# Mixers of the later chunks in another order, and the first query unit in two column parts

## The chip, the cores and the metric

The kernel runs on one core of one Trainium2 chip. The metric is the device time of one execution in microseconds (us); the median of several runs is compared. The profile is one execution, recorded by the hardware profiler. Engines: PE (TensorE, matmuls), PEld (its weight loads), DVE (VectorE), ACT (ScalarE), POOL (GpSimd, which issues the indirect gathers), SP (SyncE, which issues most plain transfers).

## The reference

One decoder layer, for 512 tokens of a prompt and 32 sample tokens (8 sequences of 4). All numbers are float32.

```
proj = x @ w_in + b_in;  q, k, v, g, ca, cg = split(proj, 6)      # D = 1024, each part 512 wide
o, r_new = retention(rope(q), rope(k), v, r0)                     # 4 heads of 128, chunks of 128 tokens
ret_out  = silu(g) * head_norm(o)
conv_out = silu(layer_norm(depthwise_conv31(ca * sigmoid(cg))))
x = layer_norm(ALPHA * x + concat(ret_out, conv_out) @ w_out)     # "mix" and LayerNorm 1
# retrieval of experts, per token:
q = (x @ w_query) as 8 heads of two halves of 128
s1, s2 = q1 @ sub_keys_1, q2 @ sub_keys_2                         # 128 keys each
take the 16 best of each, then the 16 best of their 256 sums: idx = e1*128 + e2, gate = softmax
y = sum over heads and 16: gate * gelu(u[idx] . x) * v[idx]       # 16384 experts, rows u and v of 1024
x = layer_norm(ALPHA * x + y)
```

Outputs are both token sets, the new retention states and the new convolution caches.

## The kernel before, in words

The program is written as straight Python with generators. A scheduler that simulates times then sets the order on each engine; the text gives it dependencies, priorities and a few forced orders. `behind(a, b)` forces only that `a` is issued after `b` on its engine.

*Tokens.* The first 128 prompt tokens are carried through the mixer and the retrieval early. Each of them has 8 x 16 = 128 expert slots. The other 416 tokens are the 32 samples (`NS`, columns 0 to 32) and three chunks of 128 (`C`), at columns `c0` = 0, `NS`, `NS + C`, `NS + 2C`. Their LayerNorm output is kept transposed in `x1T` (1024 x 416).

*Slots of the first 128 tokens* (`gather0`, function `gather`). For slot k, POOL gathers 128 rows of `uv` into a tile `g` (L667; u in the first half, v in the second). DVE takes the dot with x (L673), ACT makes gelu and the gated weight (L684, L685), and DVE adds weight * v to `acc` (L690). Slots up to 47 have four tiles, later ones three. The slots fill the time of other work. `hold(k, ins)` sets that the dots of slot k and later are issued behind instruction `ins`, such as the last one of a head norm (`steps["p"]`) or a LayerNorm (`steps["ln"]`).

*Mixers.* For each chunk: `retain` (scores, output and state of the retention; `advance` adds to the state `Rst`, L416, and `head_norm` makes `on`, L370), `gate_heads` (transposes of `on` at L377, product with the gate at L378), `mix_a` (the residual by a matmul with a scaled identity, L517, then 32 matmuls with `w_out`, L530: for each of two banks the convolution half first, then the gated half), and `mix_b` (LayerNorm 1 at L498 to L512, transposes into `x1T` at L553, a copy of the chunk to `x_dram`). The samples have a mix of their own, `mix_s` (L541).

*Retrieval of the 416 tokens.* For each pair of heads a "query unit" (`project`, L215) multiplies 4 x 8 blocks of `w_query` by the 416 columns of `x1T`. The result goes to `qs`; key scores (L584) and the top 16 (first MAX8 at L571) follow. The last 256 tokens are not gathered but dense: `scores_of` (L931) multiplies all expert rows `ut` by `x1T`, the chosen gates are scattered to a dense table by matmuls of one-hot tables (M, A, B, L1027 to L1058, products Ga to Gd), and `v_products` (L1115) multiplies the table with all rows `uv`. The samples ("Is", 32 slots) and the next 128 tokens ("Ib", 128 slots) are gathered like the first ones, from slot 30 of Is on only behind the `fence`, the end of the first scatter (`first_keys`). Slots are counted here through all three lists: 0 to 127 are the first tokens', 128 to 159 Is, from 160 on Ib.

*Queues and places.* SP issues the weight loads in program order; `wp` has four 1 MB places for them. `sel` is the pool of the first retrieval's scratch tiles, and of one tile `keys` of 128 x 2048 that serves as room for states and for the sums of two chunks. The room tile is kept by name `room`; `xr0` and `states` are 128 x 1024 tiles of another pool. PSUM (the matmul results) has eight banks, two groups `ps` and `ps0` given out in turn in the mixers.

Of the kernel before, what the change touches and what calls it, by code (L numbers as in the profile page):

```python
# [8 lines left out]
F32 = mybir.dt.float32  # L9
# [6 lines left out]
AF = mybir.ActivationFunctionType  # L16
# [4 lines left out]
D = 1024  # L21
# [76 lines left out]
def tile_step(ctx: ExitStack, tc: tile.TileContext, a, o):  # L98
# [5 lines left out]
    gw = ctx.enter_context(tc.tile_pool(name="gw", bufs=3))  # L104
    wps, right = ExitStack(), ExitStack()
    wp = wps.enter_context(tc.tile_pool(name="wp", bufs=4, side="right", reuse_waits="tile"))
    sel = [right.enter_context(tc.tile_pool(name="sel", bufs=2, side="right"))]
    dr = ctx.enter_context(tc.tile_pool(name="dr", bufs=1, space=bass.MemoryType.DRAM))
    front = ExitStack()
    gx = front.enter_context(tc.tile_pool(name="gx", bufs=1, reuse_waits="tile"))  # L110
# [199 lines left out]

    def conv_norm(y, n):

        pm = mmps()
        for m in range(4):
            T.matmul(pm[:, :n], onesm, y[:, m, :n], start=(m == 0), stop=(m == 3))
        pv = mmps()
        for m in range(4):
            V.tensor_sub(y[:, m, :n], y[:, m, :n], pm[:, :n])
            sq = small("sg", [128, 416], bufs=1)
            S.activation(sq[:, :n], y[:, m, :n], AF.Square)  # L320
            T.matmul(pv[:, :n], onesm, sq[:, :n], start=(m == 0), stop=(m == 3))
        rs = small("ropeB", [128, 416], bufs=1)
        S.activation(rs[:, :n], pv[:, :n], AF.Sqrt, bias=eps_c)
        V.reciprocal(rs[:, :n], rs[:, :n])
        for m in range(4):
            last = V.tensor_mul(y[:, m, :n], y[:, m, :n], rs[:, :n])
            S.activation(y[:, m, :n], y[:, m, :n], AF.Silu, bias=cg_b[:, m:m + 1], scale=cg_g[:, m:m + 1])
        return last
# [45 lines left out]
    def gate_heads(on, gT, c0):  # L374
        pt = mmps().rearrange("p (h t) -> p h t", h=H)
        for h in range(H):
            T.transpose(pt[:, h], on[:, h * DH:(h + 1) * DH], ident)  # L377
        V.tensor_mul(gT[:, :, c0:c0 + C], gT[:, :, c0:c0 + C], pt)  # L378
# [141 lines left out]
    def mix_mm(gT, y, c0, wo, xT=None):  # L520

        banks_ = [mmps(), mmps()]
        if xT is not None:
            for q in range(2):
                residual(banks_[q], xT, range(q * 4, q * 4 + 4), c0)
        for q in range(2):
            for src, k0 in ((y, 4), (gT, 0)):
                for s in range(2):
                    for k in range(4):
                        last = T.matmul(banks_[q][:, s * 256:(s + 1) * 256], src[:, k, c0:c0 + C],  # L530
                                        wo[q * 2 + s][:, k0 + k, :], start=(xT is None and k0 == 4 and s == 0 and k == 0),
                                        stop=(k0 == 0 and s == 1 and k == 3), skip_group_check=True)
        return banks_, last
# [10 lines left out]
            c = slice(j * 256, (j + 1) * 256)  # L544
            V.scalar_tensor_tensor(x1[:NS, c], x1[:NS, c], ALPHA, p[j * NS:(j + 1) * NS, 0:256], op0=OP.mult, op1=OP.add)

    def mix_norm(x1, n, x1T, c0, src=None):

        layer_norm(x1, n, ln1[0], ln1[1], src)
        for q in range(2):  # L550
            pt = mmps().rearrange("p (k t) -> p k t", k=4)
            for k in range(4):
                last = T.transpose(pt[:, k, :n], x1[:n, (q * 4 + k) * 128:(q * 4 + k + 1) * 128], ident[:n, :n])  # L553
            S.activation(x1T[:, q * 4:q * 4 + 4, c0:c0 + n], pt[:, :, :n], AF.Copy)
        return last

    def keys_or_scratch():
        return sel[0].tile([128, 2 * D], F32, name="keys", bufs=1)

    keys = []  # L560

# [168 lines left out]
    n = NR  # L730
# [55 lines left out]
    for h0 in range(0, PH, 2):  # L786
        w = load_w(a["w_query"], h0 * 256)
        qq = small("qe", [128, 4, 128], bufs=1)
        for hs in ([h0], [h0 + 1]) if h0 == 0 else ([h0, h0 + 1],):
# [43 lines left out]
    rope(load_win(1), 1, xT, n - NS, 160, [(0, n - NS, kT)])  # L833
    wg = load_win(3)
    S.activation(y[:, :, s_], yS, AF.Copy)
    hold(47, conv_norm(y, n))
    banks[:] = [ps0]
    ons = {}

    def before(c):  # L840
        c0 = C * (c - 1)
        return scores(qT, kT, c0), k_tokens(kT, c0)
# [6 lines left out]

    retain(1, *before(1))  # L850
    retain(2, *before(2))
    hold(48, steps["p"])
    banks[:] = [ps]
    silu_gate(wg, xT, n - NS, [(0, n - NS, gT[:, :, r])], False)
    wo = load_w(a["w_out"], 0) + load_w(a["w_out"], 512)
# [1 line left out]
    banks[:] = [ps, ps, ps0, ps, ps0, ps, ps, ps0]  # L857
    xrs, pms, room = {}, {}, keys_or_scratch()

    def mix_a(c0, m, place):  # L860
        xrs[c0] = fe.tile([128, D], F32, name="xr0") if place is None else room[:, place * D:(place + 1) * D]
        if c0:
            pms[c0], _ = mix_mm(gT, y, c0, wo, x1T)
            return
        x1, pms[c0] = xrs[c0], None
        nc.scalar.dma_start(x1[:m], a["x"][128:128 + m])
        mix_s(x1, gT, y, wo)

    def mix_b(c0, m):
        mix_norm(xrs[c0], m, x1T, c0, pms[c0])  # L870
        if c0 < NG2:
            nc.sync.dma_start(x1_dram[c0:min(c0 + m, NG2)], xrs[c0][:min(m, NG2 - c0)])

    gate_heads(ons[1], gT, NS)
    third = before(3)
    caches()
    mix_a(0, NS, None)
    retain(3, *third)
    hold(52, steps["p"])
    gate_heads(ons[2], gT, NS + C)  # L880
    mix_a(NS, C, 0)
    gate_heads(ons[3], gT, NS + 2 * C)
    mix_b(0, NS)
    hold(54, steps["ln"])
    mix_a(NS + C, C, 1)
    mix_b(NS, C)
    hold(56, steps["ln"])
    mix_a(NS + 2 * C, C, None)
    mix_b(NS + C, C)
    hold(59, steps["ln"])  # L890
    mix_b(NS + 2 * C, C)
    hold(60, steps["ln"])
    gather0 = gather(x1_0, I0, g0_gates, acc0, range(PH * TK))
    for _ in range(KX):
        next(gather0)
# [41 lines left out]
    qs = {}  # L937
    q_at = lambda c0, w: lambda h, s: qs[h // 2][:, h % 2 * 2 + s, c0:c0 + w]
    DG = ((0, 128), (128, ND - 128))
    qs[0] = rk.tile([128, 4, n], F32, name="qs", bufs=2)  # L940
    load_keys(pool=rk)

    for h0 in range(0, PH, 2):
        w = load_w(a["w_query"], h0 * 256)
        qs[h0 // 2] = qs[0] if h0 == 0 else rk.tile([128, 4, n], F32, name="qs", bufs=2)
        for m in range(4):
            S.activation(qs[h0 // 2][:, m], project(w, m, x1T, 0, n), AF.Copy)
        for h in (h0, h0 + 1):
# [311 lines left out]
```

## Time and profile before

| | |
|---|---|
| runs, median (lowest to highest) | 1494.05 us (1492.89 to 1497.37), 3 runs |
| profiled execution, its own time | 1502.06 us |
| its span | 1500.1 us |
| busy: PE, DVE, ACT, POOL | 1416.1 (94%), 1168.5 (78%), 499.7 (33%), 421.3 (28%) us |
| bytes moved | 503.63 MB, 336 GB/s mean |
| granted PE clock, mean | 0.971 |
| chain that ended last | PE 52%, DVE 21%, DMA 16%, ACT 5%, issue 5% |

How to read it: a row of the timeline gives the start, the length, the engine, the line, the operation with what it writes and reads, the shape and the count; in brackets stands how long the engine was idle before it and what released it. In this trace every float32 matmul has two records, so a count of 64 is 32 matmuls. A row of waits gives the total, the number of times and the longest. PEclk is the clock granted to PE as a share of full speed. The stages by time: projections, first chunk and its retrieval to about 300 us; mixers of the later chunks 300 to 420; query units and top 16 from 416, to about 685; scatter and dense scores to 920; products to the end.

### The profile page before, as it was taken

What the parts mean: (1) busy time and instruction counts of PE and PEld (TensorE: products, weight loads), DVE (VectorE), ACT (ScalarE), POOL (GpSimd) and SP (SyncE); (2) the same over time, 40 slices, a digit from 0 to 9 for tenths busy, and PEclk for the clock granted to TensorE, in tenths of its full rate; (3) what the DMA queues carried; (4) which work ended last, traced back from release to release, by engine and by line L of the source; (5) the groups of instructions that cost most, each with busy time, mean ns of one, the idle gap of its engine ahead of it and who ended that gap; (6) DMA issues with size and microseconds to landing.
All of it is one profiled execution on the core that took longest, in us unless ns stands there. A gap on an engine that the chain in (4) does not pass through costs nothing.

```text
span 1500.1 us, 19507 instructions
## 1 busy us (share of the span) xinstructions
PE 1416.1 (94%) x6602; PEld 959.1 (64%) x6602; DVE 1168.5 (78%) x2874; ACT 499.7 (33%) x1496; POOL 421.3 (28%) x397
## 2 busy tenths in 40 slices
PE   8899899987799999998999999997999999999998
PEld 7878455556657668887888775443454656666443
DVE  5839857989646999998879987677988766666665
ACT  1424763362112231254455443113673111111110
POOL 1261213335322222223232220244333332222320
PEclk9999899998999999999999999998999999999999
DMA  9749659987998779999899894899999999999995
GB/s 346 294 172 387 233 192 367 362 296 236 348 353 314 260 270 344 348 365 357 328 330 370 317 339 169 344 423 415 340 368 387 408 409 402 409 407 406 411 415 193
DMA packets 99537, 503.63 MB, mean 336 GB/s; under 512 B 10183, under 2 KB 21191, under 8 KB 56549
## 3 DMA queue, kind: packets, MB, share of 16 engines
q0 software_dynamic: 42240, 305.12, 52.6%
q1 hardware_dynamic: 52157, 190.10, 33.6%
q10 hardware_dynamic: 5040, 7.16, 1.4%
q8 instruction: 52, 0.85, 0.2%
q14 instruction: 48, 0.39, 0.1%
HBM read 496.97 MB, written 5.80 MB: 335 GB/s over the span
## 4 chain that ended last, share of the span: by engine, by line
PE 52%; DVE 21%; DMA 16%; ACT 5%; issue 5%; POOL 1%; DVEq 0%; SPq 0%; ACTq 0%; POOLq 0%
PE pB L1115 23%; PE sp L931 12%; PE mm L215 10%; DMA g<-in_uv_dram,I 5%; DVE acc L690 5%; DVE g L673 5%; DMA g<-in_uv_dram,Ib 5%; DMA g<-in_uv_dram,Is 4%; ACT blk L281 2%; PE mm L336 1%; PE mm L1058 1%; PE mm L292 1%; PE mm L530 1%; POOL g L667 1%; DVE B L1042 1%
## 5 line engine op out<-in xcount | busy, mean ns | idle before, releaser
L931 PE MATMUL sp<-x1T,uv 128*128 128x256 f32 x2048 | 470.1, 385 | 2.1 <-ACT Gc L1073 0.8
L673 DVE SCALAR_TENSOR_TENSOR g<-g,x 128x1024 f32<-128x1024 f32 x288 | 351.2, 1220 | 105.5 <-DMA g<-in_uv_dram,Ib 44.1
L931 PEld LDWEIGHTS sp<-x1T,uv 128*128 128x128 f32 x2048 | 387.3, 192 | 70.3 <-issue 15.5
L690 DVE SCALAR_TENSOR_TENSOR acc<-g,wgt,acc 128x1024 f32<-128x1024 f32 x285 | 365.3, 1282 | 85.9 <-ACT wgt L685 84.8
L667 POOL DMA_INDIRECT g<-in_uv_dram,I x128 | 161.8, 1264 | 429.2 <-DVE acc L690 228.5
L667 POOL DMA_INDIRECT g<-in_uv_dram,Ib x128 | 160.9, 1257 | 360.0 <-PE pB L1115 131.5
L684 ACT ACTIVATE act<-act 128x1 f32<-128x1 f32 x288 | 57.7, 201 | 585.2 <-DVE g L673 584.8
L215 PE MATMUL mm<-x1T,w 128*128 128x384 f32 (+1 forms) x512 | 176.2, 503 | 0.0
L1115 PE MATMUL pB<-uv,Ga 128*128 128x512 f32 x352 | 158.7, 596 | 0.0
L215 PEld LDWEIGHTS mm<-x1T,w 128*128 128x128 f32 x512 | 97.3, 191 | 74.3 <-issue 41.6
L1115 PE MATMUL pB<-uv,Gb 128*128 128x512 f32 x256 | 111.9, 595 | 0.8 <-DMA uv<-in_uv_dram 0.4
L1115 PEld LDWEIGHTS pB<-uv,Ga 128*128 128x128 f32 x352 | 65.5, 190 | 70.1 <-issue 65.0
L1115 PE MATMUL pB<-uv,Gd 128*128 128x512 f32 x256 | 110.0, 592 | 0.0
L1115 PEld LDWEIGHTS pB<-uv,Gb 128*128 128x128 f32 x256 | 47.9, 190 | 62.8 <-issue 55.4
L1115 PEld LDWEIGHTS pB<-uv,Gd 128*128 128x128 f32 x256 | 48.6, 190 | 60.8 <-issue 58.8
L667 POOL DMA_INDIRECT g<-in_uv_dram,Is x32 | 40.2, 1257 | 141.2 <-DVE Ga L1087 31.9
L1034 ACT ACTIVATE off<-row,e1T 128x128 bf16<-128x128 bf16 x256 | 78.4, 390 | 1.8 <-PE mm L1058 1.4
L1115 PE MATMUL pB<-uv,Gc 128*128 128x512 f32 x160 | 75.0, 614 | 0.1
L1058 PEld LDWEIGHTS <-A 128*128 128x128 f16 x1024 | 45.3, 97 | 44.2 <-issue 26.2
L1058 PE MATMUL mm<-B,A 128*128 128x96 f16 (+1 forms) x1024 | 49.4, 192 | 19.9 <-DVE B L1042 8.9
L215 PE MATMUL mm<-g,w 128*128 128x160 f32 (+1 forms) x512 | 67.0, 292 | 0.5 <-ACT score L586 0.5
L1071 ACT ACTIVATE W<-sp 128x256 f32<-128x256 f32 (+26 forms) x84 | 26.6, 316 | 120.8 <-PE sp L931 102.9
(302 smaller groups left out, 1571.2 us busy)
## 6 DMA issues: line engine op xcount, KB each, us to landing
uv<-in_ut_dram SPq DMA_DIRECT2D x128, 512.0 KB
uv<-in_uv_dram SPq DMA_DIRECT2D x128, 512.0 KB
w<-in_w_in_dram SPq DMA_DIRECT2D x18, 1024.0 KB
w<-in_w_query_dram SPq DMA_DIRECT2D x16, 1024.0 KB
w<-in_w_out_dram SPq DMA_DIRECT2D x7, 1024.0 KB
g<-in_uv_dram,I POOLq DMA_INDIRECT x128, 8.2
g<-in_uv_dram,Ib POOLq DMA_INDIRECT x128, 9.5
x1T<-in_xT_dram ACTq DMA_DIRECT2D x1, 1536.0 KB
```

Of the source, the lines that this page charges most:

```text
L215: T.matmul(p[:, :n], w[m // 2][:, k, (m % 2) * 128:(m % 2 + 1) * 128], xT[:, k, c0:c0 + n], start=(k == 0), stop=(k == 7))
L281: S.activation(rows[j * 32:j * 32 + 32, g], u_p[g * 32:g * 32 + 32, m, p0 + j:p0 + j + w], AF.Copy)
L292: T.matmul(p[g * 32:g * 32 + 32, :L], taps[:, g, k], rows[:, g, 4 * k:4 * k + L], start=(k == 0), stop=(k == 7))
L667: fetch = G.indirect_dma_start(out=t, out_offset=None, in_=a["uv"], in_offset=bass.IndirectOffsetOnAxis(ap=idx[:, k:k + 1], axis=0))
L673: dot = V.scalar_tensor_tensor(t[:, :D], t[:, :D], 1.0, x1, op0=OP.mult, op1=OP.mult, accum_out=act[:, 0:1])
L684: S.activation(act[:, 1:2], act[:, 0:1], AF.Gelu)
L690: V.scalar_tensor_tensor(acc, v, wgt, acc, op0=OP.mult, op1=OP.add)
L931: mm = T.matmul(sp[:, i], u[:, k], x1T[:, k, NG2:], start=(k == 0), stop=(k == 7), skip_group_check=True)
L1034: S.activation(off[:, t], row, AF.Abs, bias=e1T[:, t1 + t:t1 + t + 1])
L1058: mm = T.matmul(pt[:, t % nt], A[t % TB], B[:, q, t % TB // 2, :, t % 2], start=(q == 0), stop=(q == 1))
L1071: S.activation(W[:, :n], sp[:, :n], AF.Gelu)
L1115: return [T.matmul(pB[b][q], W[:, b * 128:(b + 1) * 128], vt[:, q * 512:(q + 1) * 512], start=False, stop=(e == NK - 1), skip_group_check= ...
```

## The change

The mixers of the later tokens come in another order: chunk 1 first, ahead of the caches and of chunk 3's retention; then chunk 2 and chunk 1's LayerNorm; then the samples, chunk 3, and the LayerNorms of samples, chunk 2 and chunk 3. The first query unit's 288 columns of samples, chunks 1 and 2 are computed ahead of the last chunk's transposes (which are forced behind the second of its four parts), its last 128 columns after them. For that its weights are loaded before chunk 2's mix, one of the two into a place that is free already. The later loop skips this unit. The dots are bound at slots 44, 45, 47, 49, 53 and 55, where they were bound at 47, 48, 52, 54, 56, 59 and 60. The scratch of the first retrieval is closed after it; the room tile and the first unit's queries get pools of their own in its place, and the queries of later units alternate between two single tiles.

```diff
+    first.close()
+    qp = ExitStack()
+    qs0 = qp.enter_context(tc.tile_pool(name="qp", bufs=1, side="right", reuse_waits="tile")).tile([128, 4, n], F32, name="qs")
+    scratch[0] = right.enter_context(tc.tile_pool(name="kp", bufs=1, side="right", reuse_waits="tile"))
...
-    hold(47, conv_norm(y, n))
+    hold(44, conv_norm(y, n))
...
-    hold(48, steps["p"])
+    hold(45, steps["p"])
...
     gate_heads(ons[1], gT, NS)
     third = before(3)
+    mix_a(NS, room[:, 0:D])
     caches()
-    mix_a(0, NS, None)
     retain(3, *third)
-    hold(52, steps["p"])
+    hold(47, steps["p"])
     gate_heads(ons[2], gT, NS + C)
-    mix_a(NS, C, 0)
+    wq = load_w(a["w_query"], 0, [kept[0], None])
+    mix_a(NS + C, room[:, D:])
+    mix_b(NS, C)
+    hold(49, steps["ln"])
+    xrs[0], pms[0] = fe.tile([128, D], F32, name="xr0"), None
+    nc.scalar.dma_start(xrs[0][:NS], a["x"][128:128 + NS])
+    mix_s(xrs[0], gT, y, wo)
     gate_heads(ons[3], gT, NS + 2 * C)
+    mix_a(NS + 2 * C, fe.tile([128, D], F32, name="states"))
     mix_b(0, NS)
-    hold(54, steps["ln"])
-    mix_a(NS + C, C, 1)
-    mix_b(NS, C)
-    hold(56, steps["ln"])
-    mix_a(NS + 2 * C, C, None)
     mix_b(NS + C, C)
-    hold(59, steps["ln"])
-    mix_b(NS + 2 * C, C)
-    hold(60, steps["ln"])
+    hold(53, steps["ln"])
+    pq0, known = [mmps() for _ in range(4)], NS + 2 * C
+
+    def first_query(m, c0, c1):
+        for k in range(8):
+            last = T.matmul(pq0[m][:, c0:c1], wq[m // 2][:, k, (m % 2) * 128:(m % 2 + 1) * 128], x1T[:, k, c0:c1],
+                            start=(k == 0), stop=(k == 7), skip_group_check=True)
+        return last
+
+    parts = [first_query(m, 0, known) for m in range(4)]
+    mix_b(NS + 2 * C, C, parts[1])
+    hold(55, steps["ln"])
+    for m in range(4):
+        first_query(m, known, n)
+        S.activation(qs0[:, m], pq0[m][:, :n], AF.Copy)
...
     for h0 in range(0, PH, 2):
-        w = load_w(a["w_query"], h0 * 256)
-        qs[h0 // 2] = qs[0] if h0 == 0 else rk.tile([128, 4, n], F32, name="qs", bufs=2)
-        for m in range(4):
-            S.activation(qs[h0 // 2][:, m], project(w, m, x1T, 0, n), AF.Copy)
+        qs[h0 // 2] = (qs0, qs1)[h0 // 2 % 2]
+        if h0:
+            w = load_w(a["w_query"], h0 * 256)
+            for m in range(4):
+                S.activation(qs[h0 // 2][:, m], project(w, m, x1T, 0, n), AF.Copy)
```

The order on the engines moves as follows. Line numbers of the changed kernel are two to three higher in these functions: before's L377, L517, L530, L541 and L553 are its L379, L519, L532, L543 and L555, before's L498 to L512 its L500 to L514, and L673 and L690 its L676 and L693.

PE, from the transposes of chunk 1's heads (L377) on, before: the retention products of chunk 3 (L392), the caches (L476, L484), and then the samples' mix (L541).

```order
L411 MATMUL mm<-v,ktok 128x128 x4
L377 MATMUL mm<-cst_89,on 128x128 x4
L392 MATMUL mm<-blk 128x128 x4
L476 MATMUL mm<-cst_89,u_p 30x128 x4
L484 MATMUL mm<-cst_89,oT 32x128 x4
L384 MATMUL mm<-cst_89,blk 128x128 x4
L541 MATMUL mm<-w,blk 32x256 x32
```

The same place after, from the same transposes (L379):

```order
L379 MATMUL mm<-cst_89,on 128x128 x4
L394 MATMUL mm<-blk 128x128 x4
L519 MATMUL mm<-scaled,x1T 128x128 x8
L532 MATMUL mm<-w,blk 128x256 x11
L386 MATMUL mm<-cst_89,blk 128x128 x4
L532 MATMUL mm<-w,blk 128x256
L486 MATMUL mm<-cst_89,oT 32x128 x4
```

Chunk 1's residual and half of its mix now stand ahead of the caches, and the samples' mix is 22 rows further down.

PE at the end of the mixers, before (`xr` is the last chunk, `keys` the room of the two others; L215 is the first query unit):

```order
L553 MATMUL mm<-cst_89,keys 128x128 x8
L517 MATMUL mm<-scaled,x1T 128x128 x8
L530 MATMUL mm<-w,blk 128x256 x32
L553 MATMUL mm<-cst_89,keys 128x128 x8
L553 MATMUL mm<-cst_89,xr_2495 128x128 x8
L215 MATMUL mm<-x1T,w 128x416 x32
```

And after (`states` is the last chunk, `xr` now the samples; L899 is `first_query`):

```order
L519 MATMUL mm<-scaled,x1T 128x128 x8
L532 MATMUL mm<-w,blk 128x256 x32
L555 MATMUL mm<-cst_89,xr_2438 128x32 x8
L555 MATMUL mm<-cst_89,keys 128x128 x8
L899 MATMUL mm<-x1T,blk 128x288 x8
L899 MATMUL mm<-x1T,w 128x288 x2
L899 MATMUL mm<-x1T,blk 128x288 x8
L899 MATMUL mm<-x1T,w 128x288 x14
L555 MATMUL mm<-cst_89,states 128x128 x8
L899 MATMUL mm<-x1T,blk 128x128 x8
```

All 32 matmuls of the 288 columns stand between the last mix and the last transposes.

DVE around the last chunk's LayerNorm, before (L673 and L690 are the dots and sums of slots):

```order
L498 BN_STATS lst<-mm 128x6
L673 SCALAR_TENSOR_TENSOR g,act<-g,x_0_129 128x1024
L690 SCALAR_TENSOR_TENSOR acc<-g,wgt,acc 128x1024 x2
L498 BN_STATS lst<-mm 128x6
L499 BN_AGGR lmv<-lst 128x2
L507 SCALAR_TENSOR_TENSOR xr_2495<-mm,lmv,lng 128x512 x2
L512 SCALAR_TENSOR_TENSOR xr_2495<-xr_2495,lrs,lnb 128x512 x2
L673 SCALAR_TENSOR_TENSOR g,act<-g,x_0_129 128x1024 x2
```

And after:

```order
L514 SCALAR_TENSOR_TENSOR keys<-keys,lrs,lnb 128x512 x2
L676 SCALAR_TENSOR_TENSOR g,act<-g,x_0_129 128x1024 x2
L500 BN_STATS lst<-mm 128x6
L693 SCALAR_TENSOR_TENSOR acc<-g,wgt,acc 128x1024 x2
L500 BN_STATS lst<-mm 128x6
L501 BN_AGGR lmv<-lst 128x2
L509 SCALAR_TENSOR_TENSOR states<-mm,lmv,lng 128x512 x2
L514 SCALAR_TENSOR_TENSOR states<-states,lrs,lnb 128x512 x2
L676 SCALAR_TENSOR_TENSOR g,act<-g,x_0_129 128x1024 x2
```

The dot between the two statistics is gone from there, and the row after the LayerNorm is the dot of slot 55, where before it was that of slot 60. From here to the end of the first scatter five dots fewer have been issued at each place; at the fence the numbers are equal, 158. On SP the loads of two states (into the room tile) are issued behind one more load of `w_in`, and of the first unit's two blocks of `w_query` one is issued ahead of the caches' stores (into the freed place `blk`) and one between the copies of chunk 1 and of the samples to `x_dram`; before, both stood behind these.

More of the change, by code (lines that the diff above doesn't have):

```diff
@@ L106, in tile_step @@
     wp = wps.enter_context(tc.tile_pool(name="wp", bufs=4, side="right", reuse_waits="tile"))
-    sel = [right.enter_context(tc.tile_pool(name="sel", bufs=2, side="right"))]
+    first = ExitStack()
+    sel = [first.enter_context(tc.tile_pool(name="sel", bufs=2, side="right"))]
+    scratch = [sel[0]]
     dr = ctx.enter_context(tc.tile_pool(name="dr", bufs=1, space=bass.MemoryType.DRAM))
@@ L545, in mix_s, with mix_norm @@
             V.scalar_tensor_tensor(x1[:NS, c], x1[:NS, c], ALPHA, p[j * NS:(j + 1) * NS, 0:256], op0=OP.mult, op1=OP.add)
-    def mix_norm(x1, n, x1T, c0, src=None):
+    def mix_norm(x1, n, x1T, c0, src=None, after=None):
         layer_norm(x1, n, ln1[0], ln1[1], src)
@@ L552, in mix_norm @@
             for k in range(4):
-                last = T.transpose(pt[:, k, :n], x1[:n, (q * 4 + k) * 128:(q * 4 + k + 1) * 128], ident[:n, :n])
+                mm = T.transpose(pt[:, k, :n], x1[:n, (q * 4 + k) * 128:(q * 4 + k + 1) * 128], ident[:n, :n])
+                if after is not None:
+                    behind(mm, after)
             S.activation(x1T[:, q * 4:q * 4 + 4, c0:c0 + n], pt[:, :, :n], AF.Copy)
-        return last
     def keys_or_scratch():
-        return sel[0].tile([128, 2 * D], F32, name="keys", bufs=1)
+        return scratch[0].tile([128, 2 * D], F32, name="keys", bufs=1)
     keys = []
@@ L858, in tile_step, with mix_a, mix_b @@
     xrs, pms, room = {}, {}, keys_or_scratch()
[L860 to L870, printed above, removed]
+    def mix_a(c0, place):
+        xrs[c0] = place
+        pms[c0], _ = mix_mm(gT, y, c0, wo, x1T)
+    def mix_b(c0, m, after=None):
+        mix_norm(xrs[c0], m, x1T, c0, pms[c0], after)
         if c0 < NG2:
@@ L939, in tile_step @@
     DG = ((0, 128), (128, ND - 128))
-    qs[0] = rk.tile([128, 4, n], F32, name="qs", bufs=2)
+    qs1 = rk.tile([128, 4, n], F32, name="qs")
     load_keys(pool=rk)
     for h0 in range(0, PH, 2):
-        w = load_w(a["w_query"], h0 * 256)
-        qs[h0 // 2] = qs[0] if h0 == 0 else rk.tile([128, 4, n], F32, name="qs", bufs=2)
-        for m in range(4):
-            S.activation(qs[h0 // 2][:, m], project(w, m, x1T, 0, n), AF.Copy)
+        qs[h0 // 2] = (qs0, qs1)[h0 // 2 % 2]
[3 more added lines that the diff above has]
+                S.activation(qs[h0 // 2][:, m], project(w, m, x1T, 0, n), AF.Copy)
         for h in (h0, h0 + 1):
@@ L954, in tile_step @@
                 retrieve(fresh(q_at(NG2 + c0, m)), range(h0 - 2, h0 + 2), m, eg[:, g], eg[:, 2 + g], h0 - 2)
+    qp.close()
     wps.close()
```

## The prediction

> **What bounds the kernel now.** I read the busy time by stretches first, then TensorE's waits, then rows of the timeline, then the chain.
>
> ```profile
> core 0: us, PE busy (x) PEld busy (x) DVE busy (x) ACT busy (x) POOL busy (x), PEclk, DMA share, GB/s
> 475.00:700.00 225.00, 219.06 (x998) 177.01 (x997) 212.00 (x725) 70.36 (x202) 57.29 (x46) 0.98 0.87 320
> 700.00:900.00 200.00, 191.85 (x1196) 164.36 (x1195) 178.35 (x393) 94.94 (x385) 51.75 (x41) 0.98 0.91 341
> 900.00:920.00 20.00, 19.62 (x105) 12.70 (x104) 12.36 (x41) 5.94 (x22) 1.04 (x1) 1.00 0.32 99
> 920.00:1060.00 140.00, 130.54 (x369) 56.75 (x368) 109.50 (x299) 36.73 (x103) 47.53 (x32) 0.96 0.91 363
> 1060.00:1495.00 435.00, 432.16 (x1657) 241.70 (x1655) 313.93 (x535) 113.30 (x361) 115.76 (x98) 1.00 0.97 386
> ```
>
> From 1060 us on TensorE is busy 432.16 of 435 us: the end is its work, and moves with whatever lets it start earlier. From 475 to 920 two engines are nearly full: TensorE idles 14.5 us, VectorE 13.0 + 21.65 + 7.64 = 42.3 us. The mixers, 300 to 420, hold TensorE's largest waits of one place:
>
> ```profile
> PE mm L553 <- DVE xr L512: 16.6, 2, 11.8
> PE mm L541 <- ACT ktok L386: 3.8, 1, 3.8
> PE mm L377 <- ACT on L370: 3.0, 1, 3.0
> PE mm L384 <- DVE Rst L416: 2.6, 1, 2.6
> ```
>
> That is 26.0 us. TensorE's rows there (start, length, idle before in brackets):
>
> ```profile
> 323.77 0.60 PE L377 MATMUL mm<-cst,on 128*128 128x128 f32 x4
> 342.11 1.95 PE L517 MATMUL mm<-scaled,x1T 128*128 128x128 f32 x16
> ...
> 366.29 0.48 PE L377 MATMUL mm<-cst,on 128*128 128x128 f32 x1 [2.97 <-ACT on L370]
> 367.26 2.08 PE L517 MATMUL mm<-scaled,x1T 128*128 128x128 f32 x8
> 369.13 3.12 PE L530 MATMUL mm<-w,blk 128*128 128x256 f32 x8
> 388.06 13.98 PE L530 MATMUL mm<-w,blk 128*128 128x256 f32 x64
> 401.88 1.04 PE L553 MATMUL mm<-cst,keys 128*128 128x128 f32 x8
> 414.69 1.94 PE L553 MATMUL mm<-cst,xr 128*128 128x128 f32 x8 [11.78 <-DVE xr L512]
> 416.46 24.05 PE L215 MATMUL mm<-x1T,w 128*128 128x416 f32 x64
> 445.44 22.61 PE L215 MATMUL mm<-x1T,w 128*128 128x416 f32 x64
> ```
>
> The last mix ends at 402.0, its LayerNorm at 415.2, and TensorE stands in front of the transposes meanwhile. After each long idle the same work is slower: 24.05 for 22.61 (+1.4), 1.94 for 1.04 (+0.9), 3.12 for 8 x 13.98/64 = 1.75 (+1.4), 2.08 for 8 x 1.95/16 = 0.98 (+1.1): 4.8 us more that belong to the waits.
>
> Why that LayerNorm is late, and the next stage, show on VectorE:
>
> ```profile
> 338.14 0.68 DVE L378 TENSOR_TENSOR blk<-blk,mm 128x512 f32<-128x512 f32 x1
> ...
> 406.95 1.23 DVE L673 SCALAR_TENSOR_TENSOR g<-g,x 128x1024 f32<-128x1024 f32 x1 [5.01 <-DMA g<-in_uv_dram,I]
> 415.12 1.22 DVE L673 SCALAR_TENSOR_TENSOR g<-g,x 128x1024 f32<-128x1024 f32 x1
> 471.21 1.25 DVE L673 SCALAR_TENSOR_TENSOR g<-g,x 128x1024 f32<-128x1024 f32 x1 [0.28 <-DMA g<-in_uv_dram,I]
> 474.64 0.49 DVE L571 MAX8 vf<-score 128x8 f32<-128x128 f32 x2 [2.17 <-ACT score L586]
> 898.33 1.22 DVE L673 SCALAR_TENSOR_TENSOR g<-g,x 128x1024 f32<-128x1024 f32 x1
> 919.73 1.22 DVE L673 SCALAR_TENSOR_TENSOR g<-g,x 128x1024 f32<-128x1024 f32 x1
> ```
>
> The dot at 406.95 waited 5.01 us for its gathered rows with the LayerNorm's second statistics queued behind it. Slot 60 runs at 415.12, slot 71 at 471.21: 5.1 us a slot. Retrieval (the first MAX8) starts at 474.64 behind 72 slots. The dot at 919.73 is the first behind the fence. From there to the TensorE-bound end the work hangs on gathers:
>
> ```profile
> PE mm L1058 <- DVE B L1042: 8.9, 2, 6.4
> ```
> ```profile
> 1030.33 10.95 DMA g<-in_uv_dram,Ib
> ```
>
> The first row is TensorE's wait in 900 to 1060, for the rows of the gathered chunk; the second is the last of a line of gathers in the chain, ahead of it. So everything after the fence moves with the fence, and I follow the gain up to there.
>
> **The change part by part.**
>
> *Mixers reordered.* The 26.0 us of waits and 4.8 of slow restarts go from their places. Two go for sure by order: the sample product L541 no longer heads the chain, and the last transposes have 64 records of the query unit's 288 columns ahead: 22.61 x 288/416 = 15.7 us, more than the 13.2 from 402.0 to 415.2. What is late next: the first mix now follows chunk 2's output. From 324.2 (after L377) TensorE has the transposes of chunk 3 (0.9), the residual (1.8), the convolution half of the mix (7.0) and small head products (2.6): 336.2. The gated half needs the product of 338.14 + 0.68, so 2.6 us of wait. The wait for chunk 3's normalised output (3.0) I let stand, since its attention now goes behind half a mix. Copies of x1T ahead of the first query columns: between 0 and the 2.17 that the MAX8 at 474.64 waited for such a copy; I take 1. New waits 6.6, lead 30.8 - 6.6 = 24.2 us at the end of the first unit. None of these is long enough that a slow restart would be sure; if one stays, the lead is 2.5 less.
>
> [...]
>
> *Query unit in columns, 416 into 288 + 128.* Same products, 64 more weight loads. The residual row has 128 columns with new weights each: 1.95/16 = 0.12 a record at most, so 64 records are 7.1 to 7.8; 15.7 + 7.1 = 22.8 against 22.61. Between 0 and +0.9; I take 0.2, on the path.
>
> [...]
>
> *Early query weights, and queues.* wq's 2 MB are asked for earlier on SP, one into a freed place, and no bytes are added. The rest of w_query still follows. What the transfer takes from gathers in the mixers is in the rivals. The state loads move behind one more weight load:
>
> ```profile
> 142.87 1.41 SPq L422 DMA_DIRECT2D keys<-in_state_retention_dram  x2
> 194.98 0.34 SPq L142 DMA_DIRECT2D w<-in_w_in_dram  x1
> 203.43 0.65 PE L456 MATMUL mm<-keys,on 128*32 128x128 f32 x16
> ```
>
> They had 60 us and now have about 8 before their use. 1 MB at the 310 to 390 GB/s of the stretches above takes 3 to 4 us: between 0 and +4, from landing at 203 or behind gathers; I take 1, late on TensorE and through to the end. POOL's gathers keep their number.
>
> *Places and banks.* The room of chunk sums in `kp`, `states` and `xr0`, the query copies in `qs0` and `qs1` used in turn, as two buffers of one pool were, and the state store before `states` is written again: I cost these at nothing, because those stores stand in SP's queue ahead of the last projection weights, and the places are taken only when these are used up. Four banks now hold the query columns until the copies. The last transposes need two others, last read by the sums of chunk 2, whose LayerNorm is ahead; if they had to wait for the first copy instead, 128 columns would stand still for 1 to 2 us. ScalarE, 70 of 225 us busy in the first stretch shown, has room for the copies.
>
> *Dots bound at lower slots.* 55 dots instead of 60 ahead of the last LayerNorm, 67 instead of 72 ahead of retrieval, and five fewer until the scatter ends. Cost of one:
>
> ```profile
> L673 DVE SCALAR_TENSOR_TENSOR g<-g,x 128x1024 f32<-128x1024 f32 x288 | 351.2, 1220 | 105.5 <-DMA g<-in_uv_dram,Ib 44.1
> L690 DVE SCALAR_TENSOR_TENSOR acc<-g,wgt,acc 128x1024 f32<-128x1024 f32 x285 | 365.3, 1282 | 85.9 <-ACT wgt L685 84.8
> ```
>
> With 0.08 for the read of the accumulator, 1.22 + 0.08 + 1.28 = 2.58 us; five are 12.9 us owed in 475 to 920.
>
> Now the lead of retrieval. TensorE alone would let it start at 474.6 - 24.2 = 450.4. The slots: of the waits 26.0 - 11.8 = 14.2 lie before the end of the last mix, and 2.5 of the slow restarts; less the new 5.6 it ends 11 earlier, at 391. Two pairs of dots and sums (5.2) and the LayerNorm's own passes (about 3, twice the 1.41 of one) follow, so slot 55 runs near 399. Twelve slots then precede MAX8: at 5.1 us, 460. In the old stretch VectorE waited
>
> ```profile
> DVE g L673 <- DMA g<-in_uv_dram,I: 24.1, 11, 5.0
> DVE acc L690 <- ACT wgt L685: 19.6, 11, 3.7
> ```
>
> and the 19.6 lay behind ScalarE's evictions of the query units, which now come earlier: without half of it a slot takes 5.1 - 0.9 = 4.2 us and MAX8 would come at 450, where TensorE allows it. So the lead is between 14.4 and 24; I take 18. Of the 12.9 owed, between none and all fits into the 42.3 us of VectorE's idle time; I take 8, since much of that idle time is itself waiting for gathers. End: -18 + 4.9 + 0.2 + 1 = -12; with the chance that the debt is smaller, since in 337 to 475 VectorE sat idle 24.1 + 19.6 us for these very slots, I take -13. Bounds: -24 (all of the lead, nothing owed, nothing for front and split) and -14.4 + 12.9 + 0.9 + 4 = +3.4.
>
> The profiled execution took 1502.06 us, span 1500.1, 8.0 above the median 1494.05. The sum gives 1489 for it, 1481 for the median.
>
> **Rivals.** 0.3% (4.5 us) is about what a measurement of this kernel can tell from no change.
>
> *The whole lead carries through.* All owed slots fit VectorE's 42.3 idle us, and retrieval starts 18 to 24 earlier: 1494.05 - 20 = 1474. For it: TensorE's own work is unchanged, and the waits gone are not VectorE's. Against: the two engines alternate in the scatter, so idle time is not free to move.
>
> *The debt eats it.* Slots keep 5.1 us: lead 14.4 less 12.9 and less 1.2 for the front and the split: 1494. Then the change does less than it says, TensorE only waiting later: its waits before the fence grow from some 14 by 20. For it: VectorE is busy 212 of 225 us behind MAX8.
>
> *Slower: bunched loads slow the gathers.* After the last LayerNorm three buffers carry the slots, while query weights and key loads come bunched. Before, one gather there was issued and used so:
>
> ```profile
> 409.65 1.94 POOL L667 DMA_INDIRECT g<-in_uv_dram,I  x1 [7.11 <-DVE acc L690]
> ```
> ```profile
> 421.06 1.23 DVE L673 SCALAR_TENSOR_TENSOR g<-g,x 128x1024 f32<-128x1024 f32 x1 [4.71 <-DMA g<-in_uv_dram,I]
> ```
>
> 11.4 us. If the pace falls to 5.6 us a slot, MAX8 comes at 399 + 67.2 = 466.2, 8.4 earlier, and the debt of 12.9, not hidden because idle time is these very waits, leaves +4.5: 1498.5. From 5.6 a slot on it decides. Against: the early wq load takes bytes out of that stretch.
>
> **How the numbers follow.** Likeliest (-8 to -18; own range 1476 to 1486): 0.47, 1481. Whole lead: 0.20, 1474. Debt eats it: 0.20, 1494. Slower: 0.13, 1498.5 and more. The range takes in the first three, 1470 (the bound of -24) to 1497 (the bound of +3.4). Faster by over 0.3%: 0.47 + 0.20 = 0.67; within: 0.20; slower: 0.13.
>
> **What would show it.** TensorE's waits in 300 to 420 fall under 10 us, the transposes of the last chunk wait for nothing, the first unit's 128 columns end near 416. First MAX8 near 456; the fence's dot near 907. Should MAX8 be early and the fence not, the owed slots were mis-sized; if MAX8 stays later than 466, the gathers' pace was. If the waits for ACT or VectorE reappear at the second or third gated half, the lead was.

## The result and the profile after

| | before | after |
|---|---|---|
| median of 12 runs each | 1497.59 us (1490.77 to 1503.94) | 1488.87 us (1481.6 to 1494.9) |
| profiled execution, span | 1502.06, 1500.1 us | 1488.64, 1486.7 us |
| busy PE, DVE | 1416.1, 1168.5 us | 1415.3, 1168.2 us |

The ratio of the runs is 0.9934, 95% interval 0.9908 to 0.9960: 0.7% faster, some 10 us (6 to 14). The three runs known ahead had a median of 1494.05; with nine more of the same kernel it is 1497.59. One kernel's runs spread over 13 us, so single traces below are read for where time goes, and the medians for how much.

Both engines are as busy as before; only idle time went. TensorE's waits in 300 to 420 (kernel after):

```profile
PE mm L899 <- ACT x1T L558: 4.5, 2, 3.2
PE mm L323 <- ACT sg L322: 1.8, 1, 1.8
PE mm L532 <- DVE blk L380: 0.7, 1, 0.7
```

7.0 us where 26.0 stood. The waits for the LayerNorms are gone, and the largest that is left is new: the query columns (L899) wait for copies of x1T. TensorE's rows there:

```profile
330.98 0.60 PE L379 MATMUL mm<-cst,on 128*128 128x128 f32 x4
...
392.55 4.15 PE L899 MATMUL mm<-x1T,blk 128*128 128x288 f32 x16 [1.23 <-ACT x1T L558]
...
408.17 1.04 PE L555 MATMUL mm<-cst,states 128*128 128x128 f32 x8
412.45 3.79 PE L899 MATMUL mm<-x1T,blk 128*128 128x128 f32 x16 [3.25 <-ACT x1T L558]
416.03 1.49 PE L899 MATMUL mm<-x1T,w 128*128 128x128 f32 x6
...
419.60 3.07 PE L899 MATMUL mm<-x1T,w 128*128 128x128 f32 x26
422.50 0.61 PE L587 MATMUL mm<-keys,qs 128*128 128x128 f32 x4
```

The 288 columns took 392.55 to 408.17 = 15.6 us and the last transposes behind them waited for nothing. The first row is chunk 1's head transposes, at 323.77 before: TensorE entered the mixers 7.2 us later, and still had the first scores at 422.50 instead of 440.35, where the kernel before has them:

```profile
440.35 0.61 PE L584 MATMUL mm<-keys,qs 128*128 128x128 f32 x4
```

VectorE: the first MAX8, the last dot ahead of the fence, the last multiplication of the scatter (L1105), whose end is the fence, and the first dot behind it.

```profile
453.67 0.89 DVE L574 MAX8 vf<-score 128x8 f32<-128x128 f32 x4 [2.15 <-ACT score L589]
...
898.92 1.23 DVE L676 SCALAR_TENSOR_TENSOR g<-g,x 128x1024 f32<-128x1024 f32 x1 [1.73 <-DMA g<-in_uv_dram,Is]
...
905.62 0.33 DVE L1105 SCALAR_TENSOR_TENSOR Ga<-mm,Ga 128x176 f32<-128x176 f32 x1
...
906.20 1.22 DVE L676 SCALAR_TENSOR_TENSOR g<-g,x 128x1024 f32<-128x1024 f32 x1
```

Retrieval starts 21.0 us earlier (474.64), the fence is 13.5 earlier (919.73), the span 13.4 shorter. Behind the fence both kernels take 580.5 us. So 7.5 of the 21 us are lost between 454 and 906. Busy time by stretch, after:

```profile
core 0: us, PE busy (x) PEld busy (x) DVE busy (x) ACT busy (x) POOL busy (x), PEclk, DMA share, GB/s
416.00:475.00 59.00, 58.84 (x274) 43.43 (x273) 41.69 (x127) 14.82 (x46) 14.97 (x12) 0.98 0.90 348
475.00:700.00 225.00, 218.41 (x1027) 177.52 (x1026) 210.69 (x668) 74.37 (x230) 62.94 (x48) 0.98 0.87 326
700.00:900.00 200.00, 187.79 (x1165) 157.42 (x1164) 175.58 (x386) 89.98 (x362) 51.67 (x41) 0.99 0.91 335
920.00:1060.00 140.00, 133.69 (x429) 57.75 (x428) 109.42 (x282) 40.30 (x109) 51.02 (x35) 0.96 0.94 374
```

VectorE is no busier in 475 to 900 than before (386.3 of 425 us, 390.4 before), while TensorE idles 12.2 us in 700 to 900 instead of 8.2: it came early and waits there. VectorE's work up to 475 us, before and after:

```profile
core 0: us, DVE busy (x), PEclk, DMA share, GB/s
0.00:475.00 475.00, 340.61 (x886) 0.94 0.81 299
...
0.00:475.00 475.00, 350.18 (x970) 0.96 0.80 302
```

Up to the fence VectorE does the same work in both kernels, 742.8 and 742.3 us. So the 13.5 us are idle time of VectorE that is gone: 9.6 ahead of 475 (134.4 to 124.8) and 3.5 between 475 and the fence (42.3 to 38.8). This sum says where the time went, and not what made it go.

### The profile page after: what moved, and what is told of

Read it like the earlier page. It is cut to its first block, busy times and chain, and to the rows that moved or that the text cites. A ratio compares the mean times of both kernels' runs of the same rounds, so it can differ in the third digit from the quotient of the medians.

```text
span 1486.7 us, 19633 instructions
## 1 busy us (share of the span) xinstructions
PE 1415.3 (95%) x6666; PEld 966.0 (65%) x6666; DVE 1168.2 (79%) x2874; ACT 498.8 (34%) x1496; POOL 426.3 (29%) x397
## 4 chain that ended last, share of the span: by engine, by line
PE 46%; DVE 23%; DMA 17%; issue 7%; ACT 4%; POOL 2%; ACTq 0%; SPq 0%; DVEq 0%; POOLq 0%
PE pB L1133 22%; PE sp L947 13%; DMA g<-in_uv_dram,I 7%; PE mm L217 7%; DVE acc L693 6%; DVE g L676 5%; DMA g<-in_uv_dram,Ib 5%; DMA g<-in_uv_dram,Is 4%; ACT blk L283 2%; PE mm L1076 1%; PE mm L532 1%; POOL g L670 1%; DVE iu L575 1%; PE mm L899 1%; DVE B L1060 1%
## 5 line engine op out<-in xcount | busy, mean ns | idle before, releaser
L693 DVE SCALAR_TENSOR_TENSOR acc<-g,wgt,acc 128x1024 f32<-128x1024 f32 x285 | 365.1, 1281 | 86.9 <-ACT wgt L688 85.3
L676 DVE SCALAR_TENSOR_TENSOR g<-g,x 128x1024 f32<-128x1024 f32 x288 | 350.7, 1219 | 94.2 <-DMA g<-in_uv_dram,Ib 39.9
L670 POOL DMA_INDIRECT g<-in_uv_dram,I x128 | 166.4, 1300 | 438.5 <-DVE acc L693 209.0
L217 PE MATMUL mm<-x1T,w 128*128 128x384 f32 (+1 forms) x448 | 152.5, 498 | 0.0
L217 PEld LDWEIGHTS mm<-x1T,w 128*128 128x128 f32 x448 | 84.4, 190 | 62.9 <-issue 30.8
L1133 PE MATMUL pB<-uv,Gb 128*128 128x512 f32 x256 | 115.1, 602 | 5.8 <-DMA uv<-in_uv_dram 4.1
```

The lines of the kernel that those rows point to most:

```text
L217: T.matmul(p[:, :n], w[m // 2][:, k, (m % 2) * 128:(m % 2 + 1) * 128], xT[:, k, c0:c0 + n], start=(k == 0), stop=(k == 7))
L670: fetch = G.indirect_dma_start(out=t, out_offset=None, in_=a["uv"], in_offset=bass.IndirectOffsetOnAxis(ap=idx[:, k:k + 1], axis=0))
L676: dot = V.scalar_tensor_tensor(t[:, :D], t[:, :D], 1.0, x1, op0=OP.mult, op1=OP.mult, accum_out=act[:, 0:1])
L693: V.scalar_tensor_tensor(acc, v, wgt, acc, op0=OP.mult, op1=OP.add)
L1133: return [T.matmul(pB[b][q], W[:, b * 128:(b + 1) * 128], vt[:, q * 512:(q + 1) * 512], start=False, stop=(e == NK - 1), skip_group_check= ...
```

## The experiments

Three theories were set against each other. A: VectorE's work bounds the stretch up to the fence, and the change wins VectorE's idle time ahead of it. B: the slots are a clock; from slot 76 (501.2 and 500.3) to 157 (898.3 and 898.9) they run at the same times in both kernels, and the scatter is early because fewer slots stand ahead of it. C: TensorE's waits in the mixers are the gain.

**Old slots in the changed order.** Edit of the changed kernel:

```diff
-    hold(44, conv_norm(y, n))     # likewise 45 -> 48, 47 -> 52, 49 -> 54, 53 -> 58, 55 -> 60
+    hold(47, conv_norm(y, n))
```

> The changed order of mixers and the column parts, with the dots bound at the slots of the kernel before (47, 48, 52, 54, 58, 60): 58 dots instead of 55 stand ahead of the last LayerNorm, 108 instead of 106 ahead of the scatter. Theory A (what is won is VectorE's idle time ahead of 475 us, 41.7 us busy in 416 to 475 instead of 27.8; slots only change places): the end stays within 4 us of the changed kernel, 7 to 12 below the kernel before. Theory B (the slots are a clock: from slot 76 on they run at the same times in both kernels, 4.9 us each, and the scatter is early only because five fewer slots stand ahead of it): two slots more ahead of the scatter put it about 10 us later, and the gain is gone, within 3 us of the kernel before. Theory C (TensorE's waits in the mixers are the gain): as A, less what TensorE waits again at the last transposes, 5 to 10 below.

Measured: 1483.49 us, ratio 0.9908 (0.9872 to 0.9945). B falls: with two slots more ahead of the scatter it is no slower than the changed kernel, and its median is 5 us lower; the intervals overlap, so whether it is faster is not shown. The ratio puts it 8 to 19 us below the kernel before, about 14: more than A (7 to 12) and C (5 to 10) had named, and not clearly outside of either. In this order and with the column parts, the lower slots are not what gains. TensorE waits again, for the gated half of a mix and at the samples' transposes, and it does not show at the end:

```profile
PE mm L532 <- DVE blk L380: 3.1, 1, 3.1
PE mm L555 <- DVE xr L514: 3.0, 1, 3.0
```

**Lower slots alone, in the order of before.**

```diff
-    hold(47, conv_norm(y, n))     # likewise 48 -> 45, 52 -> 47, 54 -> 49, 56 -> 51, 59 -> 53, 60 -> 55
+    hold(44, conv_norm(y, n))
```

> The kernel before, with the dots bound at 44, 45, 47, 49, 51, 53 and 55 alone: 55 dots ahead of the last LayerNorm, 107 ahead of the scatter; order of mixers as before, no column parts. A: the last LayerNorm no longer stands behind a gather, TensorE gets some 5 of its 11.8 us of wait back, VectorE as many: end 3 to 5 us below the kernel before. B: nearly the whole gain of the change, 8 to 10 below. C: 0 to 5 below.

Measured: 1497.61 us, 0.9989 (0.9965 to 1.0012): no change that can be told, and at most 5 us. B (8 to 10) falls here too; of the 3 to 5 us of A and the 0 to 5 of C the interval leaves room for both. Yet in its trace, from the slowest of its twelve executions, TensorE's waits in the mixers had fallen:

```profile
PE mm L541 <- ACT ktok L386: 3.8, 1, 3.8
PE mm L553 <- DVE xr L512: 2.8, 1, 2.8
PE mm L384 <- DVE Rst L416: 2.6, 1, 2.6
PE mm L377 <- ACT on L370: 1.0, 1, 1.0
```

10.2 instead of 26.0 us, the first scores at 424.7, MAX8 at 463.8, and the fence at 917.3 against 919.7. C falls in its plain form: 16 us of TensorE's waits and an 11 us earlier retrieval were worth at most 5 us. In this trace 8.4 of the 10.8 us of lead were gone at the fence, with 69 slots instead of 72 ahead of MAX8 (three are 7.7 us of VectorE's work): the prediction's rival in which the debt eats the lead, in a kernel of its own.

**No column parts.**

```diff
-    parts = [first_query(m, 0, known) for m in range(4)]
-    mix_b(NS + 2 * C, C, parts[1])
+    mix_b(NS + 2 * C, C)
...
-        first_query(m, known, n)
+        first_query(m, 0, n)
```

> The changed kernel with the first query unit whole again (416 columns behind the last transposes), its weights still loaded early. TensorE should wait some 7 us at the last transposes (the LayerNorm ends at 398.9, the matmuls ahead of it at 391) and be 5 us later at the first scores. A: the first MAX8 5 us later, the end 3 to 5 above the changed kernel. B: as the changed kernel, since the slots stand where they stood. C: 5 to 7 above the changed kernel.

Measured: 1488.03 us, 0.9945 (0.9920 to 0.9971), as the changed kernel. That is what B had named; A had 3 to 5 us above it and C 5 to 7. The two ratios differ by 1.6 us and are each known to about 4, so A's figure is not excluded, and not borne out. The wait is there as expected, and cost nothing that can be measured:

```profile
399.04 1.94 PE L555 MATMUL mm<-cst,states 128*128 128x128 f32 x8 [7.05 <-DVE states L514]
```

First scores at 425.4 (422.5 with parts), MAX8 at 456.2 (453.7), the dot behind the fence at 900.4 (906.2): retrieval 2.5 us later, the fence 5.8 earlier.

**State loads held back, in the kernel before.**

```diff
-                load_states(b, r0, nc.sync)
+                await_(load_states(b, r0, nc.sync), last_idx[0])   # last copy of the first retrieval's indices
```

> The kernel before with its two state loads held back until the first retrieval has its last indices (193 us), as the room forces in the changed kernel. If the front's delay (the changed kernel is 7.2 us later at 293 us) comes from these loads and carries through: 5 to 7 us above the kernel before. If it comes from them and is absorbed: TensorE 3 to 7 us later at 293, the end within 2. If the delay has another source: no change at 293 either.

Measured: 1502.42 us, 1.0024 (0.9997 to 1.0051): +3.6 us by the ratio, with an interval that reaches zero. TensorE's first use of these states stayed at 203.65 (203.43), so it did not wait for the loads there; but a row of the later projections, the first L321 past 290, came at 298.3 instead of 293.5. In the lower-slots kernel, whose front is that of before, it is at 295.8; in the changed kernel and the seven others with its front and whole dots at 297.8 to 300.9, mean 299.4 (with half dots, an experiment below, at 296.4). So some 2 us are spread between runs and some 5 (299.4 less the mean of 293.5 and 295.8) belong to the changed front. Holding the loads back gives about as much, 3.7, from one trace; but the scheduler also reorders TensorE's rows there, so that the loads are the cause is possible and not shown.

**Half of each dot.** VectorE multiplies 512 of 1024 columns per slot (half of each product is left out); gathers and TensorE's work stay.

```diff
-            dot = V.scalar_tensor_tensor(t[:, :D], t[:, :D], 1.0, x1, ...
+            dot = V.scalar_tensor_tensor(t[:, :512], t[:, :512], 1.0, x1[:, :512], ...
```

> The changed kernel with each slot's dot over 512 of its 1024 columns: VectorE has some 0.6 us less per slot, 48 us less in the 81 slots between 475 and 898, while gathers, transfers and TensorE's work stay. Its output is not the reference's, since half of each product is left out. Theory A (VectorE's work bounds that stretch): the slots draw together, the dot behind the fence comes 12 to 25 us earlier than 906 (TensorE, idle only 21 us of that stretch, then holds it), the end with it. Theory B2 (the loop of three gather buffers bounds it): slot 157 stays within 5 us of 899, and the end within 4 us of the changed kernel.

Measured, in two executions: 1465.08 us, 0.9790 (0.9756 to 0.9825), by the ratios some 22 us below the changed kernel. VectorE:

```profile
475.00:700.00 225.00, 220.59 (x1091) 182.53 (x1090) 190.45 (x631) 80.41 (x254) 54.34 (x52) 1.00 0.93 352
700.00:900.00 200.00, 193.68 (x1132) 156.25 (x1131) 164.16 (x443) 91.77 (x360) 41.43 (x36) 0.98 0.87 321
```

It is 31.7 us less busy in 475 to 900 (354.6 against 386.3). Slot 157 runs at 874.5 instead of 898.9, the dot behind the fence at 882.7 instead of 906.2, and the end is 22.8 earlier in the trace. That is inside A's range, and outside B2's, under which the loop of three gather buffers fixes the slots' times. But the run does not tell VectorE's load from that loop, because the dot is a step of it. In the changed kernel the gather of slot k+3 is issued 0.27 us (median; never less) after the sum of slot k has freed its buffer, so one lap serves three slots: 14.8 us, where the half dots have 14.2. A dot is 0.53 us shorter (1.219 to 0.686). Over the 81 slots from 76 to 157, VectorE's work alone would give 81 x 0.53 = 43 us, the loop a third of it, 14.4; measured are 15.0, and the other 9.4 had come by slot 76 (490.9 for 500.3). Against a pure loop speaks that only 22 of the changed kernel's dots in 475 to 900 waited for their rows, 22.3 us in all: most rows lay ready while VectorE did something else. What bounds the stretch is both in turn, as far as this shows.

**Slots five lower still.** Holds 39, 40, 42, 44, 48, 50.

> The changed kernel with the dots bound five slots lower still (39, 40, 42, 44, 48, 50): 101 slots instead of 106 ahead of the scatter. TensorE's waits in the mixers cannot fall much further (7 us left). A: five more slots, 12.9 us of VectorE's work, are owed behind 475 and little is won ahead: 3 to 12 us above the changed kernel. If instead lower slots were what gains, the end falls again by about as much as the change gained, 8.

Measured: 1495.57 us, 0.9990 (0.9970 to 1.0010): 0.0056 x 1497.6 = 8.4 us above the changed kernel, in the range that A gave, and not for A's reason. TensorE's waits in the mixers fall to the copies (1.9 us) and MAX8 comes at 449.3, the earliest of all with whole dots; but slot 40 runs at 339.0 instead of 324.1, and slot 157 at 916.6 instead of 898.9. The scatter was not late:

```profile
898.55 0.33 DVE L1105 SCALAR_TENSOR_TENSOR Ga<-mm,Ga 128x176 f32<-128x176 f32 x1
...
899.66 1.22 DVE L676 SCALAR_TENSOR_TENSOR g<-g,x 128x1024 f32<-128x1024 f32 x1 [0.43 <-DMA g<-in_uv_dram,Is]
...
907.77 1.23 DVE L676 SCALAR_TENSOR_TENSOR g<-g,x 128x1024 f32<-128x1024 f32 x1 [3.87 <-DMA g<-in_uv_dram,Is]
...
912.91 1.23 DVE L676 SCALAR_TENSOR_TENSOR g<-g,x 128x1024 f32<-128x1024 f32 x1 [2.03 <-DMA g<-in_uv_dram,Is]
...
916.64 1.23 DVE L676 SCALAR_TENSOR_TENSOR g<-g,x 128x1024 f32<-128x1024 f32 x1 [0.61 <-DMA g<-in_uv_dram,Is]
...
919.86 1.23 DVE L676 SCALAR_TENSOR_TENSOR g<-g,x 128x1024 f32<-128x1024 f32 x1
```

The fence is at 898.9, 7 us ahead of the changed kernel's 906.0, with 154 slots ahead of it instead of 158. The four slots that did not get there, 154 to 157, run behind it and wait for their rows, 20.2 us up to the dot of slot 158. Slots held back by 15 us in the mixers are not caught up: the slots were late, and the scatter was not.

**Four slots moved behind the fence**, with the old slots (`FREE = 26` for 30).

> The changed order with the old slots (58 ahead of the last LayerNorm), and four of the samples' slots moved behind the fence (FREE 26 instead of 30). A: 10 us of VectorE's work leave the stretch ahead of the fence, which comes 5 to 10 us earlier; behind it VectorE has 30 us idle of 140, so half of that may reach the end: 3 to 6 below the variant with the old slots (1483.5). If the slots behind the fence follow one another at the gathers' pace of 3.9 us, the four give 15 us back, and the end is 0 to 6 above that variant.

Measured: 1493.82 us, 0.9987 (0.9965 to 1.0008), 10 above the kernel with the old slots; more than the worse of the two expected cases. The first dot behind the fence, now that of slot 154, runs at 900.4, where slot 158 had 902.6: the 10 us of VectorE's work that left the stretch brought the fence 2.2 us forward, and A had 5 to 10. Slot 160 runs at 948.8 instead of 934.8: 14.0 us for four slots, 3.5 each. From the end of the scatter to slot 160 it is 48.7 us for 32.5 (52.4 for 34.4 in the kernel with slots five lower still): four slots more behind the fence take 16 to 18 us, 4 and more each, where VectorE's work on one is 2.58.

**Old slots without column parts.**

> The changed order and the early weights alone: old slots, and the first query unit whole behind the last transposes. TensorE waits there for the last LayerNorm, some 12 us (slot 58 runs near 410, and 15.7 us of query columns no longer cover it). A: VectorE has the same work done by 475 if its first MAX8 is not held up by TensorE; that comes about 6 later than 456.6, and the end 0 to 6 above the variant with the old slots and parts (1483.5). C (TensorE's waits): 10 above it.

Measured: 1499.12 us, 1.0022 (1.0002 to 1.0043), 0.0114 x 1497.5 = 17 above the same slots with the parts: worse than both theories said. TensorE waits for both LayerNorms:

```profile
PE mm L555 <- DVE xr L514: 7.2, 1, 7.2
PE mm L555 <- DVE states L514: 4.8, 1, 4.8
```

First scores at 431.1 (425.6 with parts), MAX8 7.2 later, scatter behind 111 slots instead of 108, fence 7.4 later (910.0 against 902.6). That goes with 7 to 10 us (its span is 10.5 longer); its profiled execution, at 1491.58, is the fastest of its twelve, so what makes the rest of 17 stays open.

**Two more places for slots.** All 32 sample slots ahead of the fence, with the old slots (`FREE = 32`); and a middle set of holds in the changed kernel (47, 48, 49, 51, 55, 57).

> The changed order with column parts and the old slots (58 ahead of the last LayerNorm), and all 32 sample slots ahead of the fence instead of 30. Behind the fence a slot costs 3.7 us of the chain (160 to 184 in 94 us of the kernel before), ahead of it 2.58 us of VectorE: two slots should win about 2 us on the variant with 30 (1483.5), so 1480 to 1485. If slots ahead of the fence cost their gather's time as well, 0 to +4.

> The changed kernel with the dots bound at 47, 48, 49, 51, 55 and 57: 57 slots ahead of the last LayerNorm, 106 ahead of the scatter as in the changed kernel, where the old slots give 58 and 108. If what the old slots win (1483.5 against 1488.9) is the VectorE work of the slots owed behind 475 us: between the two, nearer the changed kernel, 1485 to 1489. If it is the number of slots ahead of the last LayerNorm alone: as the old slots.

Measured: 1484.61 us, 0.9928 (0.9902 to 0.9955), and 1490.64 us, 0.9960 (0.9947 to 0.9974). The first is not told apart from 30 slots (its 3.7 us for a slot behind the fence is 94 us over 24 slots, so 3.9). The second lies with the changed kernel, slightly above what was expected; it has 57 slots ahead of the last LayerNorm and 106 ahead of the scatter, so one slot fewer ahead of the LayerNorm than with the old slots does not give their time; what favours them is not shown.

All kernels with whole dots and `FREE = 30`, by trace and ratio:

| kernel | VectorE busy by 475 us | slots ahead of the scatter | dot behind the fence, us | ratio |
|---|---|---|---|---|
| before | 340.6 | 111 | 919.7 | 1 |
| lower slots alone | 344.7 | 107 | 917.3 | 0.9989 |
| slots five lower still | 343.7 | 101 | 899.7 (slot 154) | 0.9990 |
| old slots, no parts | 349.4 | 111 | 910.0 | 1.0022 |
| changed | 350.2 | 106 | 906.2 | 0.9934 |
| middle slots | 351.4 | 106 | 906.6 | 0.9960 |
| no parts | 349.9 | 108 | 900.4 | 0.9945 |
| old slots | 348.8 | 108 | 902.6 | 0.9908 |
| state loads held back | 337.7 | 110 | 917.2 | 1.0024 |

Every kernel that is clearly faster had 348 us or more of VectorE's work done by 475 and the dot behind the fence by 907. The reverse does not hold: the old slots without parts had the work done and are not faster, and the slots five lower still had the earliest fence and are not either, since four slots were left behind it. A is borne out in part: the idle time that is gone is VectorE's, but A named too much for the lower slots alone, for the kernel without parts and for the fence with four slots moved, where it had 5 to 10 us and 2.2 came. That VectorE's time alone bounds the stretch is not shown.

The parts of the change can be told apart by the medians. The order with early weights is no gain alone (1.0022), and neither are the lower slots (0.9989). The order with the lower slots (0.9945), with the column parts (0.9908) or with both (0.9934) is. TensorE's waits in the mixers are 14.9 us in the first of these, 10.2 in the second and 7.6, 8.1 and 7.0 in the last three; but the slots five lower still have under 2 and no gain, so these waits do not decide it by themselves. Against the kernel before, the changed order with the old slots is the best median of these (1483.49 us, 0.9908); its interval overlaps that of the changed kernel.

## Why the prediction was right

The direction held, and so did the path up to the fence: TensorE's waits went, retrieval began earlier, and part of that lead was lost on the way. What sets how much arrives was argued in the prediction and is still open. 1481 was forecast for the median and 1488.87 measured, outside the 1476 to 1486 of the likeliest case and inside the whole range, 1470 to 1497. Of the 7.9 us between the medians 3.5 come from the base, since the kernel before has 1497.59 over twelve runs, and 4.3 from a gain of 8.7 where 13 stood, which is inside the 8 to 18 of the likeliest case. That the profiled execution came out at 1488.64 for 1489 is luck: the profiled execution of the kernel before is 4.5 us above its median of twelve, that of the changed kernel is not, so the two traces differ by 13.4 where the medians differ by 8.7.

- *TensorE's waits.* 26.0 to 7.0 us, under the 10 named. New waits were priced 6.6: the gated half waited 0.7 for 2.6, since TensorE came 7 us later itself (the sum up to that half adds to 336.5 and not 336.2, so 2.3), the heads' output 0 for 3.0, and the copies of x1T 4.5 for 1. A wait of 1.8 at L323 was not priced.
- *Slow restarts.* That no new wait was long enough for a slow restart to be sure was too kind, and the 2.5 us named for one was right: after the 3.25 us wait 16 records of 128 columns took 3.79 us and six more 1.49, at the pace of the last 26 (3.07/26 = 0.118) 1.89 and 0.71: 2.7 us lost, on top of the wait (all 64 records took 10.23 us, where that pace gives 7.55). The granted clock was 1.00 in the transposes ahead of that wait and 0.50 from 412.45 to 418.20, 5.75 us. In the kernel before, the wait of 2.97 us at 366.29 already had 0.50 behind it, up to 371.00 at least; behind the 1.23 us at 392.55 the changed kernel had 1.00. How long a wait must be for this is not shown.
- *Split into columns.* Priced 0.2 by the residual rows. At that full pace, 64 records at 0.118 are 7.6 us, and 15.6 + 7.6 = 23.2 against 22.61: +0.6, inside the 0 to 0.9 given.
- *Front.* Mis-sized most: +1 taken, bounds 0 to +4. TensorE entered the mixers 7.2 us late, some 5 of it from the changed front, past the upper bound. The sum looked only at the first use of the two states, which came 2.8 later (206.20), not at the order of the rest of the front. It was partly hidden: TensorE's lead at the first scores was 17.9 (24.2 forecast, 422.5 instead of 416), but MAX8 was within 2.3 us of its forecast (453.7; 456).
- *Owed slots.* The lead of retrieval was 21.0 for 18, and 7.5 of it was lost up to the fence for 4.9 charged: 60% of the 12.9 us owed. The fence's dot was forecast at 907 and ran at 906.2, two misses of about 3 us that cancel. The size of the debt did not hold in the other traces: the middle slots lost 9.6 of 12.9, the lower slots alone 8.4 where 7.7 was owed, but the old slots 0.9 of the 10.3 for four slots, and the kernel without parts nothing. So a lead can be lost here, its size was not known better than none to all, and the 4.9 fell well by luck. The kernel with slots five lower still paid in another place, behind the fence.
- *Everything behind the fence moves with it.* For this pair it held, 580.4 and 580.5 us from the dot behind the fence to the end of the span, and 581.2 with half dots. It is no rule: the other traces with 30 slots ahead of the fence have 576.4 (old slots) to 585.6 (lower slots alone), and the two with 154 slots ahead of the fence have some 590 (899.7 to 1489.6, 900.4 to 1491.2).
- *Rivals.* The whole lead did not carry: 7.5 of 21 were lost. The debt ate most of the lead in the kernel with the lower slots alone. The slowing of gathers did not come: from slot 55 (398.8) to 66 (450.3), the last ahead of MAX8, a slot took 4.7 us, under the 5.6 and a little under the 5.1 of before. The prediction's working priced twelve steps of 5.1 for these eleven and the 3.4 us from the last dot to MAX8 (453.67 - 450.3), so its least lead, 14.4, was 1.7 too small.

## What to carry to other kernels

Here two engines are both nearly full in one stretch (475 to 900 us in the changed kernel: TensorE 406.2, VectorE 386.3 of 425), and with the lower slots alone 16 us less of TensorE's waits ahead of it were worth at most 5: take the busy time of both up to the start of such a stretch, in each variant, before pricing a wait. Run the parts of a change one by one as well: here neither the order nor the lower slots gained alone, and together they did. Background work that is held back to let an urgent step pass is a debt, of which the traces here paid none to all: count the slots at each join, since a join that comes earlier can leave some of them behind it, where they cost more (here 3.5 to 4.5 us each, for 2.58 of VectorE's work). A step that is moved into freed room can take that room's last reader along as a wait (here some 5 us of the front are late, and the loads as their cause are not shown), and the rest of that stage's order should be priced with it, not the first use alone.

## What had not been expected of the hardware

A slot is 2.58 us of VectorE's work (dot 1.22, read of its sum 0.08, addition 1.28), and that was its price nowhere: four slots fewer ahead of the fence brought the fence 2.2 us forward with the old slots, and four more behind it put slot 160 back by 14.0. Three gather buffers were not a clock of fixed times: with half the dot the same 81 slots from 76 to 157 took 383.6 us (490.9 to 874.5) instead of 398.6, a third of what VectorE was spared on 81 dots, as in a loop of three buffers that contains the dot. And a wait of 3.25 us came with a granted clock of 0.50 on TensorE from 412.45 to 418.20, 5.75 us of work, where behind one of 1.23 us (392.55) the clock was 1.00 and the next 16 records took 4.15 us against 4.04 later.
